# Inverse roots of two norms: from small products and a chain on VectorE to a sum by ones and ScalarE's reciprocal root

## The chip, the cores and the metric

The kernel runs on one core of a Trainium2 chip. The metric is the device time of one launch in microseconds (us), as the median of several runs. The profile is one more execution, recorded by the hardware profiler; its time stands beside the others below.

A core has a matrix engine (TensorE, PE in the profile, with its weight loads as PEld), an elementwise engine (VectorE, DVE), a function engine (ScalarE, ACT), GpSimd (POOL) and SyncE (SP), whose queue issues most of the DMAs here. TensorE writes into PSUM, eight banks of 128 partitions by 512 float32 columns. Each engine works through a queue of its own in order, and waits on semaphores where it needs another's result.

## The reference, cut to what matters

A decoder layer over 2048 tokens of width 1024: a norm, a mixing part (a gated recurrence in four heads beside sliding-window attention), an output projection, a second norm, a gated feed-forward part of width 2816 with a short convolution, and a final norm.

```python
def rmsnorm(x, w, eps=EPS):
    xf = x.astype(jnp.float32)
    inv = lax.rsqrt(jnp.mean(xf * xf, axis=-1, keepdims=True) + eps)
    return (xf * inv * w.astype(jnp.float32)).astype(x.dtype)
...
        h = h + mix @ w_out[l]
        v = rmsnorm(h, norm_ffn_w[l])
        gate = causal_depthwise_conv(v @ w_gate[l], conv_w[l], conv_b[l])
        h = h + (jax.nn.silu(gate) * (v @ w_up[l])) @ w_down[l]
    return rmsnorm(h, final_norm_w)
```

The inverse root "inv" is one number for each token. It is computed for x, for h (after the mixing part) and for the result (the final norm).

## The kernel before, in words

**Layout.** Activations are kept transposed: features on the 128 partitions, tokens along the columns. A token's inverse root therefore multiplies a whole column, and has to stand on all 128 partitions.

**Order of the work.** The tokens are done in two halves of 1024 (hf 0 and 1). Each half runs the mixing part, then `out_proj` (products "pop"), `gate_up` (11 pairs of feature tiles, a gate pair and an up pair each) and `down`. Large products are made in float32r, each factor split into a high and a low part, with three products in place of one; the splits are a cast on ScalarE and a subtraction on VectorE (L721 and L722, or L195 and L196). The feed-forward products use a seven-product scheme for 2x2 blocks: `pair_unit` makes the products A11, A12, S2, S1, S3, S4 and A22 and gathers them in the banks X, Z and Y. X and Y take up further products on top of what they hold, so each is first copied away by ScalarE ("s", "u", L903). Usually the order is A11 into X, A12 into Z, S2 on top of X. The very first gate pair of a half, which follows on `out_proj`, has the order A11, A12, S1, S2, S4, S3, A22, and a new X for A22.

**The planner.** The program is written as tiles and operations, and a planner orders the instructions in each engine's queue by readiness and the order in the program, and hands out the buffers. What stands later in the code may run earlier. A name such as "mm" is a ring of buffers: PSUM has four banks "mm", two "hg" and two "at". The ring "ut" has seven buffers of 128x512 float32 in SBUF.

**Sums of squares.** `Stats` gathers the squares of a stage's tiles in an accumulator `acc`, one partial sum per partition and token. `inverse` (L258 on) makes inverse roots from it: for each 128 tokens a product with the 128x128 block of `acc` as weights and one column of ones as the moving operand sums over the partitions; the sums land with tokens on partitions, in a few columns of a bank "hg" (tile pst, L271). On these, 128x8 or 128x4 elements, `rsqrt` (L164 on) runs eleven small VectorE operations: a scaled copy, a first guess from the bits, three Newton steps of three operations. Then one VectorE operation (L279) writes a diagonal matrix per 128 tokens into `acc`. `spread` (L281 on) multiplies 512 columns of these diagonals by a 128x128 matrix of ones (tile pinv, L289, banks "hg" and "at" in turn) which puts each inverse root on all partitions, and ScalarE copies it to `acc` (L292).

**Where they are used.** `load` and `head` make them for x (tile invb). `gate_up` makes those of h: `inverse` at the product S4 of the first gate pair, `spread` at A22, and the pending multiplications of the gate by invb (L962, `flush`) behind that. `down` makes those of the final norm, in two parts of 512 tokens: "o2" for the upper and "o" for the lower ones (tile sums in the first half). In the first half o2's `inverse` stands at the second piece of the last product P4 and its `spread` two pieces later, with `finish`, which multiplies eight tiles (L1201) and writes them out; o's `inverse` stands in the unit "kv" that already belongs to the second half, and its `spread` and `finish` in the next unit. In the second half the loop ends before these points, and the tail computes o2 and o (in two parts of 256) in its own way.

Of the kernel before, what the change touches and what calls it, by code (L numbers as in the profile page):

```python
# [8 lines left out]
F32 = mybir.dt.float32  # L9
# [3 lines left out]
AF = mybir.ActivationFunctionType  # L13
ALU = mybir.AluOpType
# [3 lines left out]
P = 128  # L18
D = 1024
# [11 lines left out]
EPS = 1e-6  # L31
# [9 lines left out]
UT = 7  # L41
# [12 lines left out]
def hymba_layer(ctx: ExitStack, tc: tile.TileContext, a: dict, out: bass.AP):  # L54
    nc = tc.nc
# [17 lines left out]
    def ps(kind, name):  # L73
        return spaces[kind].tile([P, 512], F32, tag=kind, name=name)

    aux = ("hg", "at")
# [7 lines left out]
    ones = cp.tile([P, P], F32, name="ones")  # L84
    nc.vector.memset(ones, 1.0)
    warm, eps = [t[:, i:i + 1] for t in [cp.tile([P, 2], F32, name="warm")] for i in range(2)]
# [148 lines left out]
    class Stats:  # L235
# [26 lines left out]
        def inverse(self, keep, last=None):  # L262

            n = self.acc.shape[-1]
            nt = n // P
            st = ps("hg", "pst")

            for src in (self.acc, last):
                if src is not None:
                    for c in range(nt):  # L270
                        marks["pst"] = nc.tensor.matmul(st[:, c:c + 1], src[:, c * P:(c + 1) * P], ones[:, 0:1],  # L271
                                                        start=src is self.acc and (c == 0 or last is None),
                                                        stop=last is None or src is last,
                                                        skip_group_check=last is not None)
            if last is not None:
                without_use(ps("at", "idle"), TAIL_WARM, marks["pst"])
            rs = self.rs = rsqrt(st[:, 0:nt], nt, 1.0 / D, keep, last is not None)
            dg = self.acc
            return nc.vector.tensor_tensor(dg.rearrange("p (c t) -> p c t", t=P),  # L279
                                    ident.unsqueeze(1).to_broadcast([P, nt, P]),  # L280
                                    rs.unsqueeze(2).to_broadcast([P, nt, P]), op=ALU.mult)  # L281

        def spread(self, bank=None):

# [113 lines left out]
    def first_unit(X, i, then={}, kind="mm"):  # L398
        return unit(a["w_att"][ATT_J + i], X, "kv", kind=kind, then=then)
# [544 lines left out]
    def gate_up(hf, ops, hs, nxt, last, p):  # L944

        acts = {op: [dp.tile([P, n, 512], F32, name=f"act{hf}{op}{i}") for i, n in enumerate(PIECES)] for op in OPS}
        lo, hi = slice(0, 512), slice(512, HALF)
        invb = hs.acc
        srcs = [w[2 * pr:2 * pr + 2] for pr in range(FT // 2) for w in (a["w_gate"], a["w_up"])]
        for pr in range(FT // 2):  # L950
            f0 = 2 * pr
            W, nxt = nxt, None

            ga = [p.tile([P, HALF + 64], F32, tag="ga", name="ga", bufs=2)[:, 0:2 + HALF] for _ in range(2)]

            def gate(i, j, x, y):
                dst = ga[i][:, 2 + j * 512:2 + (j + 1) * 512]
                iv = invb[:, j * 512:(j + 1) * 512]
                if y is not None:
                    nc.vector.tensor_tensor(dst, x, y, op=ALU.add)  # L960
                    x = dst
                later.append(lambda: nc.vector.tensor_tensor(dst, x, iv, op=ALU.mult))  # L962
                if pr:
                    flush()

            def flush():
                while later:
                    later.pop(0)()

            later = []  # L970
            then = {"S4": lambda: hs.inverse("h"), "A22": lambda: (hs.spread(), flush())} if pr == 0 else {}
            if pr == 0:
                def behind_first(copied):
                    nonlocal nxt
                    with behind(*last(copied)):
                        nxt = prep_pair(srcs[1][0], srcs[1][1])

                pair_unit(W, ops, p, gate, then, behind_first)
            else:
                nxt = prep_pair(srcs[2 * pr + 1][0], srcs[2 * pr + 1][1])  # L980
                pair_unit(W, ops, p, gate, then)
            flush()
            ys = []
            for i in range(2):
                ft, g = f0 + i, ga[i]
                nc.scalar.copy(g[:, 0:2], halo[:, ft])
                nc.scalar.copy(halo[:, ft], g[:, HALF:HALF + 2])
                y = slot("y")
                nc.scalar.activation(y, g[:, 2:2 + HALF], AF.Identity, scale=C.cw[:, ft, 2:3], bias=C.cw[:, ft, 3:4])  # L989
                for w in (1, 0):  # L990
                    nc.vector.scalar_tensor_tensor(y, g[:, w:w + HALF], C.cw[:, ft, w:w + 1], y,  # L991
                                                   op0=ALU.mult, op1=ALU.add)
                nc.scalar.activation(y, y, AF.Silu)
                nc.vector.tensor_tensor(y, y, invb, op=ALU.mult)
                ys.append(y)

            def up(i, j, x, y):
                dst = ys[i][:, j * 512:(j + 1) * 512]
                if y is not None:
                    nc.vector.tensor_tensor(y, x, y, op=ALU.add)  # L1000
                    x = y
                nc.vector.tensor_tensor(dst, x, dst, op=ALU.mult)

            W = nxt
            if pr + 1 < FT // 2:
                nxt = prep_pair(srcs[2 * pr + 2][0], srcs[2 * pr + 2][1])
            pair_unit(W, ops, p, up)

            y1, y2 = ys
            dst = {op: acts[op][pr // 2][:, pr % 2] for op in OPS}  # L1010
            tt = slot("T13")
            nc.sync.dma_start(dst["B11"], y1[:, lo])
            nc.sync.dma_start(dst["B21"], y2[:, lo])
            nc.sync.dma_start(dst["B22"], y2[:, hi])
            nc.vector.tensor_tensor(tt[:, lo], y1[:, hi], y1[:, lo], op=ALU.subtract)
            nc.sync.dma_start(dst["T1"], tt[:, lo])
            nc.vector.tensor_tensor(tt[:, hi], y2[:, hi], y1[:, hi], op=ALU.subtract)
            nc.sync.dma_start(dst["T3"], tt[:, hi])
            nc.vector.tensor_tensor(y1[:, lo], tt[:, hi], y1[:, lo], op=ALU.add)
            nc.sync.dma_start(dst["T2"], y1[:, lo])  # L1020
            nc.vector.tensor_tensor(y2[:, lo], y2[:, lo], y1[:, lo], op=ALU.subtract)
            nc.sync.dma_start(dst["T4"], y2[:, lo])
        return acts

    def down(hf, kept, acts, p):
# [4 lines left out]
        lo, hi = slice(0, 512), slice(512, HALF)  # L1030
        final = hf + 1 == NH
        NP = len(PIECES)
        todo = [(name, w, t, j) for name, w, t in PRODUCTS for j in range(NP)]
        S = {}

# [44 lines left out]
        hh = []  # L1080
# [32 lines left out]
        X, xs, acc = [], None, None  # L1113
        end = len(todo) - NP
        for k, (name, _, _, j) in enumerate(todo):
            if k + 2 < len(todo):
                ready[k + 2] = prep_piece(k + 2)
            if j == 0:
# [4 lines left out]
                else:  # L1123
                    o = by if name == "P3" else bx
                if name == "P3":
                    acc = inv_tile() if final else wp.tile([P, HALF], F32, tag="raw", name="sums", bufs=RAW)
                    s1, s2 = [Stats(acc[:, bs], lambda: p.tile([P, 512], F32, tag="ut", name="fsq", bufs=UT))
                              for bs in (lo, hi)]
# [3 lines left out]
            if not final and k >= end - 3:  # L1132
                xs = next(loading, xs)
            if final and k == end:
                break
            if k == end + 1:
                s2.inverse("o2")
            elif k == end + 3:
                s2.spread()
                finish(hf, hh, s2, hi, [nc.sync])  # L1140
            for d in range(4):
                product(k, o[d], d)
            if j + 1 < NP:
                continue
# [18 lines left out]
        if final:  # L1163
# [4 lines left out]
            for i, (st, bs) in enumerate(steps):  # L1168
                for d in range(4):
                    for k in range(end, len(todo)):  # L1170
                        product(k, bx[d][:, bs], d, bs)
                    t = hh[d + 4][:, bs]
# [17 lines left out]
            steps[1][0].inverse("o", last)  # L1190
            finish(hf, hh, steps[1][0], steps[1][1], [nc.scalar, nc.sync], steps[1][0].spread(1))
            return None
        kv = [first_unit(X, 0, {3: lambda: s1.inverse("o"), 7: lambda: xs.inverse("x")}, "aux")]
        kv.append(first_unit(X, 1, {2: lambda: (s1.spread(), finish(hf, hh, s1, lo, [nc.sync])), 4: xs.spread}))
        f0 = unit(a["w_f"][0], X, "f")
        return X, kv, xs.acc, xs.rs, f0

    def finish(hf, hh, st, bs, queues, inv=None):
        for d in range(KT):
            t = hh[d][:, bs]  # L1200
            nc.vector.tensor_tensor(t, t, st.acc if inv is None else inv, op=ALU.mult)  # L1201
            queues[d % len(queues)].dma_start(out[d, :, hf * HALF + bs.start:hf * HALF + bs.stop], t)

    X = []
    *nxt, summed = X, *head(X)
    for hf in range(NH):
        X, kv, invb, rs, f0 = nxt
        with ExitStack() as st:
            p = pool(f"mix{hf}", stack=st, reuse_waits="tile")
# [25 lines left out]
        with ExitStack() as st:  # L1235
            p = pool(f"ffn{hf}", stack=st, reuse_waits="tile")
            kept, ops, hs, first, last = out_proj(hf, M, p)
# [63 lines left out]
```

## Time and profile before

| | |
|---|---|
| runs | 2151.5, 2153.11, 2151.62 us; median 2151.62 |
| the profiled execution | 2152.56 us, span 2150.8 us |
| granted clock of TensorE | 0.999 |
| instructions | 28224 |
| matrix products on pst (L271), records | 100: 80 from invb, 16 from sums, 4 from fsq |
| matrix products on pinv (L289), records | 26: 22 from invb, 4 from sums |
| spread's copy on ScalarE (L292) | 11 of 128x512 |
| table loads of ScalarE | 33 of 1283 ns |

The span runs from the first to the last instruction. A row of a timeline has the start in us, the length in us, the engine, the line of the code, the operation, output and inputs, shapes and a count; what stands in brackets is the idle time before it and what ended it. Products overlap, so the length of one (0.39 us for 128x512) is more than the distance to the next. A float32 product (one that isn't float32r) leaves two records. In a table of stretches the columns are the stretch, its length, the busy time and the number of instructions of PE, PEld, DVE, ACT and POOL, the granted clock, the share of the DMA engines and GB/s. In a table of groups stand the busy time, the mean length of one in ns, and the idle time before them with what ended it.

### The profile page before, as it was taken

How to read it: one execution, taken by the hardware profiler on the slowest of the kernel's cores; microseconds unless marked ns; L12 is line 12 of the kernel's file. 1: busy time of each engine (PE TensorE's matmuls, PEld its weight loads, DVE VectorE, ACT ScalarE, POOL GpSimd, SP SyncE). 2: the span in 40 equal slices, each digit the busy share in tenths (PEclk: the TensorE clock that was granted, in tenths of full speed). 3: DMA queues.
4: the chain of work that ended last, by engine and by line, in shares of the span. 5: the costliest groups of instructions: out<-in, count | busy, mean ns of one | idle time of the engine just before them, and what ended most of it. 6: DMA issues, size and time to landing. Idle time of an engine off the chain costs nothing.

```text
span 2150.8 us, 28224 instructions
## 1 busy us (share of the span) xinstructions
PE 2136.1 (99%) x10752; PEld 1786.6 (83%) x10752; DVE 1662.3 (77%) x2450; ACT 1091.3 (51%) x1858; POOL 6.0 (0%) x28
## 2 busy tenths in 40 slices
PE   9999999999999999999999999999999999999998
PEld 7888888888888888888888888888888888888888
DVE  6557888798887878785864688878978788887766
ACT  6456566564444445335734576646544444443353
POOL 1000000000000000000000000000000000000000
PEclk9999999999999999999999999999999999999999
DMA  4111112513232235964631111215223323269643
GB/s 158 49 40 40 42 37 69 164 48 132 86 126 93 97 114 171 380 222 157 214 129 41 46 42 40 64 38 174 84 93 101 110 91 122 92 205 398 224 137 133
DMA packets 94383, 258.04 MB, mean 120 GB/s; under 512 B 11416, under 2 KB 17576, under 8 KB 94248
## 3 DMA queue, kind: packets, MB, share of 16 engines
q1 hardware_dynamic: 88992, 251.30, 34.5%
q10 hardware_dynamic: 5256, 4.94, 0.8%
q8 instruction: 84, 1.38, 0.3%
q14 instruction: 51, 0.42, 0.1%
HBM read 195.10 MB, written 57.15 MB: 117 GB/s over the span
## 4 chain that ended last, share of the span: by engine, by line
PE 79%; ACT 2%; DVE 2%; issue 1%; DMA 0%; ACTq 0%; DVEq 0%
PE X L896 7%; PE X L898 7%; PE X L897 7%; PE pop L217 6%; PE pdx L1109 4%; PE pdx L1107 4%; PE Y L898 4%; PE Y L897 4%; PE Y L896 4%; PE pdx L1108 4%; PE pdy L1109 3%; PE pdy L1108 3%; PE pdy L1107 3%; PE f L217 2%; PE hq L217 2%; PE q L217 2%
## 5 line engine op out<-in xcount | busy, mean ns | idle before, releaser
L721 ACT CAST whi<-raw 128x1024 fp32r<-128x1024 f32 x88 | 92.6, 1053 | 110.3 <-PE X L897 67.6
L897 PE MATMUL X<-T,whi 128*128 128x512 f32 x352 | 137.0, 389 | 0.0
L896 PE MATMUL X<-T,whi 128*128 128x512 f32 x352 | 137.0, 389 | 0.0
L898 PE MATMUL X<-T,wlo 128*128 128x512 f32 x352 | 136.9, 389 | 0.0
L991 DVE SCALAR_TENSOR_TENSOR y<-ga,cw,y 128x1024 f32<-128x1024 f32 x88 | 112.3, 1277 | 26.0 <-ACT y L989 25.9
L903 ACT COPY u<-X 128x512 f32<-128x512 f32 x88 | 51.4, 584 | 133.0 <-PE X L898 132.6
L722 DVE TENSOR_TENSOR wlo<-raw,whi 128x1024 fp32r<-128x1024 f32 x88 | 107.0, 1215 | 0.0
L195 ACT CAST whi<-raw 128x1024 fp32r<-128x1024 f32 x57 | 59.7, 1051 | 87.1 <-PE hq L217 37.1
L196 DVE TENSOR_TENSOR wlo<-raw,whi 128x1024 fp32r<-128x1024 f32 x57 | 69.4, 1217 | 43.3 <-ACT whi L195 42.8
L722 DVE TENSOR_TENSOR xld<-raw,xhd 128x1024 fp32r<-128x1024 f32 x72 | 80.5, 1129 | 19.8 <-ACT xhd L721 19.4
L721 ACT CAST xhd<-raw 128x1024 fp32r<-128x1024 f32 x72 | 69.6, 977 | 43.5 <-DMA raw<-act0T 13.9
L217 PE MATMUL pop<-XL,whi 128*128 128x512 f32 x256 | 88.6, 392 | 0.0
L217 PE MATMUL pop<-XH,wlo 128*128 128x512 f32 x256 | 87.7, 391 | 0.0
L217 PE MATMUL pop<-XH,whi 128*128 128x512 f32 x256 | 86.4, 393 | 0.0
L897 PEld LDWEIGHTS X<-T,whi 128*128 128x128 f32 x352 | 66.1, 188 | 13.7
L898 PEld LDWEIGHTS X<-T,wlo 128*128 128x128 f32 x352 | 66.1, 188 | 13.7
L896 PEld LDWEIGHTS X<-T,whi 128*128 128x128 f32 x352 | 66.0, 188 | 13.7
L1107 PE MATMUL pdx<-xhd,hid 128*128 128x512 f32 x192 | 74.5, 392 | 1.6 <-ACT hid L721 1.0
L619 DVE TENSOR_TENSOR QK<-QK,f 128x1024 f32<-128x1024 f32 x56 | 68.5, 1224 | 8.1 <-ACT G L605 7.7
L1108 PE MATMUL pdx<-xld,hid 128*128 128x512 f32 x192 | 74.7, 389 | 0.0
L1109 PE MATMUL pdx<-xhd,lod 128*128 128x512 f32 x192 | 73.8, 389 | 0.0
L896 PE MATMUL X<-T,Sh 128*128 128x512 f32 x176 | 68.7, 391 | 1.5 <-ACT s L903 1.5
(385 smaller groups left out, 6413.1 us busy)
## 6 DMA issues: line engine op xcount, KB each, us to landing
wr<-in_w_down SPq DMA_DIRECT2D x90, 512.0 KB, 5.4
raw<-in_w_gate SPq DMA_DIRECT2D x44, 512.0 KB, 3.7
raw<-in_w_up SPq DMA_DIRECT2D x44, 512.0 KB, 3.6
raw<-act0T SPq DMA_DIRECT2D x20, 512.0 KB, 8.2
raw<-act1T SPq DMA_DIRECT2D x20, 512.0 KB, 8.3
act0B<-y SPq DMA_DIRECT2D x33, 256.0 KB, 3.2
act1B<-y SPq DMA_DIRECT2D x33, 256.0 KB, 2.3
raw<-in_w_out SPq DMA_DIRECT2D x16, 512.0 KB, 5.1
```

The source lines that it names most:

```text
L196: nc.vector.tensor_tensor(lo, raw, hi.bitcast(F32), op=ALU.subtract)
L217: marks["unit"] = nc.tensor.matmul(o[b], w, x[:, bs], start=f, stop=l)
L619: done = nc.vector.tensor_tensor(own, own, Fv.rearrange("p b w -> p w b").unsqueeze(3).to_broadcast([P, 2, nb, m]), op=ALU.mult)
L721: return (nc.scalar.copy(h, src), (eng or nc.vector).tensor_tensor(l, src, h.bitcast(F32), op=ALU.subtract))
L722: (eng or nc.vector).tensor_tensor(l, src, h.bitcast(F32), op=ALU.subtract))
L896: nc.tensor.matmul(o, wh[:, ws], xh, start=i == 0 and not more, stop=False, skip_group_check=more)
L897: nc.tensor.matmul(o, wh[:, ws], xl, start=False, stop=False, skip_group_check=more)
L898: r = nc.tensor.matmul(o, wl[:, ws], xh, start=False, stop=i == 3, skip_group_check=more)
L991: nc.vector.scalar_tensor_tensor(y, g[:, w:w + HALF], C.cw[:, ft, w:w + 1], y, op0=ALU.mult, op1=ALU.add)
L1107: nc.tensor.matmul(o, wh[:, i, c], ah[:, i, cols], start=f, stop=False, skip_group_check=more)
L1108: nc.tensor.matmul(o, wh[:, i, c], al[:, i, cols], start=False, stop=False, skip_group_check=more)
L1109: nc.tensor.matmul(o, wl[:, i, c], ah[:, i, cols], start=False, stop=l, skip_group_check=more)
```

## The change

A new function `everywhere` of `Stats` takes the place of `inverse` and `spread` at h (both halves) and at o2 and o (first half). For each 512 columns it multiplies `acc` itself by the 128x128 ones, in float32, so that the sum over the partitions stands on all partitions at once. ScalarE makes a reciprocal root of it with scale and eps; VectorE scales the sums, and one Newton step follows: a square on ScalarE and two VectorE operations, the last of which writes the inverse root into `acc`. The two work tiles come from the ring "ut". The banks are "mm" for h, and "hg" for o2 and o.

```diff
+        def everywhere(self, part, kinds):
+
+            n = self.acc.shape[-1]
+            for b in range(n // 512):
+                a = self.acc[:, b * 512:(b + 1) * 512]
+                s = ps(kinds[b % 2], "psum")
+                nc.tensor.matmul(s, ones, a, start=True, stop=True)
+                y, t = part("y"), part("t")
+                nc.scalar.activation(y, s, AF.Abs_reciprocal_sqrt, scale=1.0 / D, bias=eps)
+                nc.vector.tensor_scalar(a, s, -0.5 / D, -0.5 * EPS, op0=ALU.mult, op1=ALU.add)
+                nc.scalar.activation(t, y, AF.Square)
+                nc.vector.tensor_tensor(t, t, a, op=ALU.mult)
+                nc.vector.scalar_tensor_tensor(a, t, 1.5, y, op0=ALU.add, op1=ALU.mult)
...
+        def ring(name):
+            return p.tile([P, 512], F32, tag="ut", name=name, bufs=UT)
...
-            then = {"S4": lambda: hs.inverse("h"), "A22": lambda: (hs.spread(), flush())} if pr == 0 else {}
+            then = {"S4": lambda: hs.everywhere(ring, ("mm", "mm")), "A22": flush} if pr == 0 else {}
...
             if k == end + 1:
-                s2.inverse("o2")
+                s2.everywhere(ring, aux)
             elif k == end + 3:
-                s2.spread()
                 finish(hf, hh, s2, hi, [nc.sync])
...
-        kv = [first_unit(X, 0, {3: lambda: s1.inverse("o"), 7: lambda: xs.inverse("x")}, "aux")]
-        kv.append(first_unit(X, 1, {2: lambda: (s1.spread(), finish(hf, hh, s1, lo, [nc.sync])), 4: xs.spread}))
+        kv = [first_unit(X, 0, {3: lambda: s1.everywhere(ring, aux), 7: lambda: xs.inverse("x")}, "aux")]
+        kv.append(first_unit(X, 1, {2: lambda: (finish(hf, hh, s1, lo, [nc.sync])), 4: xs.spread}))
```

The inverse roots of x, and the second half's final norm, keep `inverse` and `spread`.

More of the change, by code (lines that the diff above doesn't have):

```diff
@@ L1032, in down, with ring @@
         NP = len(PIECES)
+        def ring(name):
+            return p.tile([P, 512], F32, tag="ut", name=name, bufs=UT)
         todo = [(name, w, t, j) for name, w, t in PRODUCTS for j in range(NP)]
```

## The prediction

> **What bounds the kernel now.** I read the busy times of the page first, then the table of stretches, then the waits of TensorE, then its timeline around each place that the change touches.
>
> ```profile
> PE 2136.1 (99%) x10752; PEld 1786.6 (83%) x10752; DVE 1662.3 (77%) x2450; ACT 1091.3 (51%) x1858; POOL 6.0 (0%) x28
> 440.00:480.00 40.00, 39.27 (x177) 31.74 (x176) 35.33 (x56) 21.94 (x35) 0.00 (x0) 1.00 0.13 40
> 875.00:1040.00 165.00, 165.00 (x729) 136.64 (x728) 112.30 (x117) 74.86 (x85) 0.00 (x0) 1.00 0.68 247
> 1040.00:1112.00 72.00, 72.00 (x329) 58.65 (x328) 60.59 (x103) 40.36 (x52) 0.00 (x0) 1.00 0.54 180
> PE X L896 <- ACT s L903: 1.5, 2, 0.7
> ```
>
> TensorE is busy in all of 875 to 1040: 729 products in 165 us, one every 226 ns. Between 440 and 480 it loses 0.73 us, and the row of waits names the reason: twice in the run the up-product on bank X waits 0.7 us for ScalarE's copy "s". Whatever leaves TensorE's queue in such a stretch should come off the span. VectorE is the engine to watch: 35.33 of 40 us in the first place of the change, 60.59 of 72 in the other.
>
> **What is removed from TensorE.** Four inversions change: h in each half, o2 and o in the first. Those of x and of the second half's final norm stay. For each changed one the products on pst go (eight for h, four for o2 or o; each stands as two records), and the products on pinv stay as products of the same shape, 128x512 float32 by ones, only now on the raw sums. In the chain of waits the pieces are:
>
> ```profile
> 447.67 1.68 PE pst L271 x16
> 463.71 1.72 PE pinv L289 x4
> 1046.09 0.79 PE pst L271 x8
> 1083.05 0.79 PE pst L271 x8
> 1513.11 1.68 PE pst L271 x16
> ```
>
> All four pst pieces lie on the chain that ends last. By these rows 1.68 + 0.79 + 0.79 + 1.68 = 4.94 us go; the 1.72 us of pinv per h (0.43 a record) remains. The timeline says a little more, because the first product after pst is slow too:
>
> ```profile
> 447.28 0.39 PE L897 MATMUL Y<-B,S 128*128 128x512 f32 x1
> 447.51 1.84 PE L271 MATMUL pst<-ones,invb 128*128 128x1 f32 x16
> 449.21 0.49 PE L898 MATMUL Y<-B,S 128*128 128x512 f32 x1
> 449.53 0.40 PE L896 MATMUL Y<-B,S 128*128 128x512 f32 x1
> 1045.70 0.39 PE L1109 MATMUL pdx<-xh2d,lod 128*128 128x512 f32 x1
> 1046.73 0.49 PE L1107 MATMUL pdx<-xh2d,hid 128*128 128x512 f32 x1
> 1047.06 0.40 PE L1108 MATMUL pdx<-xl2d,hid 128*128 128x512 f32 x1
> ```
>
> From the start at 447.28 to that at 449.53 are 2.25 us, where two products at 0.226 would take 0.45: pst costs 1.80. At 1045.70 to 1047.06 it is 1.36 less 0.45, so 0.91. Twice each: 5.42 us. The direct term lies between 4.94 and 5.42.
>
> **The stall behind h.** The up-pair normally runs A11 into X, A12 into Z, then S2 on top of X, so that Z covers the copy of X. In the pair behind h the order is another:
>
> ```profile
> 459.55 0.39 PE L898 MATMUL X<-B,wlo 128*128 128x512 f32 x1
> 460.67 0.50 PE L896 MATMUL X<-T,Sh 128*128 128x512 f32 x1 [0.73 <-ACT s L903]
> 461.00 0.40 PE L897 MATMUL X<-T,Sh 128*128 128x512 f32 x1
> 463.55 1.88 PE L289 MATMUL pinv<-invb,ones 128*128 128x512 f32 x4
> 464.86 0.80 PE L896 MATMUL Z<-B,whi 128*128 128x512 f32 x1
> ...
> 460.03 0.58 ACT L903 COPY s<-X 128x512 f32<-128x512 f32 x1 [1.43 <-PE X L898]
> ...
> 461.24 1.23 DVE L279 TENSOR_TENSOR invb<-ident,y 128x1024 f32<-128x1024 f32 x1
> ```
>
> S2 comes straight after A11, and Z directly after pinv. In the code spread takes its banks from "hg" and "at", and Z is the next tile from "at": I read it so that Z's bank is handed out only after pinv's, and pinv needs VectorE's multiply, which ends at 462.5. The changed h takes both banks from "mm" and takes them 16 us earlier, at the place of pst, where the sums are done. Nothing then holds Z back, and its 2.7 us (twelve products at 0.226) lie over the copy of 0.58. What goes is 461.00 - 459.55 - 0.45 = 1.00 us by starts, 0.73 by the wait alone; twice, so 1.46 to 2.00. Below: nothing, if the order stays. I take it as gone.
>
> "mm" has four banks: X of A11, the two sums, and X of A22 fill them, and the fifth request, X of the up-pair at 457, takes the first X, which ScalarE's "u" copy of 454.59 frees in the trace of before. The sums' banks are asked for again only in the next pair, about 20 us on. I cost the bank change at nothing.
>
> **What is added on VectorE and ScalarE.** For each 512 columns VectorE gets three operations over 128x512, ScalarE a reciprocal root from PSUM and a square, and it loses the copy of pinv. The reciprocal root is in no row; its neighbours are these:
>
> ```profile
> L716 ACT ACTIVATE v<-pvv,y 128x512 f32<-128x512 f32 x16 | 11.0, 688 | 34.8 <-PE pvv L715 34.8
> L248 ACT ACTIVATE sq<-h 128x512 f32<-128x512 f32 x28 | 16.3, 622 | 0.7 <-DVE h L786 0.7
> L993 ACT ACT_TABLE_LOAD x2 | 2.6, 1283 | 0.0
> L786 DVE TENSOR_TENSOR h<-h,pop 128x512 f32<-128x512 f32 x32 | 20.4, 680 | 7.5 <-DMA h<-in_xT 6.2 <-PE pop L217 1.3
> 454.59 0.59 ACT L903 COPY u<-X 128x512 f32<-128x512 f32 x1 [4.99 <-PE X L898]
> ```
>
> For h, ScalarE's new work is a table load of 1.28 us at most (nothing, if the function shares a set with its neighbours), two roots at about 0.69 and two squares at 0.62: 3.9 us. It has a hole of 4.99 us just there, before 454.59, after the sums can be ready (447.5 + 1.72 = 449.2). The hole hides it; without it the copies "u" and "s" would be up to 3.9 us late.
>
> VectorE gets six operations at 0.68 (0.60 from start to start, 3.6 to 4.1 us) and loses eleven small ones and the 1024-wide multiply:
>
> ```profile
> 450.32 0.15 DVE L169 TENSOR_SCALAR ms<-pst 128x8 f32<-128x8 f32 x1
> 456.50 1.22 DVE L722 TENSOR_TENSOR Sl<-S,Sh 128x1024 fp32r<-128x1024 f32 x1
> 461.04 0.17 DVE L181 SCALAR_TENSOR_TENSOR y<-t,y 128x8 f32<-128x8 f32 x1
> 465.22 2.50 DVE L962 TENSOR_TENSOR ga<-ga,invb 128x512 f32<-128x512 f32 x4 [2.75 <-ACT invb L292]
> ```
>
> The small ones run from 450.32 to 461.2, squeezed between large ones, and the inverse is everywhere only at 465.22, with VectorE idle 2.75 us before it. The new chain is shorter: sums at 449.2, root and square by about 453, the last two VectorE operations by 456 to 458. So the gate multiplies move some 8 us ahead, and VectorE's hole at 462.5 fills. Net it works about 1 us more per h. What could be late is the split Sl: done at 457.7, and its first product is the third of S2, two after 460.67 at 461.2; with Z ahead, pst and the stall gone it starts at 461.2 + 2.7 - 1.8 - 1.0 = 461.1, so 3.4 us of room against at most 4.1 added ahead of it, less five small ones (0.1 each between large ones), and only if all six go ahead of Sl. I take nothing for it, and keep it for the slower rival.
>
> **o2 and o, at the end of the first half.** Per call three VectorE operations (2.0 us) for eleven small ones and a multiply of 0.68, and on ScalarE 1.3 us for one copy, with one table load for both calls. TensorE reads pieces split two ahead, so some us of delay are covered. The step that moves is the finish of o2: eight multiplies with their eight output DMAs on SP's queue.
>
> ```profile
> 1066.65 1.23 DVE L196 TENSOR_TENSOR wlo<-raw,whi 128x1024 fp32r<-128x1024 f32 x1 [0.26 <-ACT whi L195]
> 1070.53 0.68 DVE L1093 TENSOR_TENSOR h<-h,pdx 128x512 f32<-128x512 f32 x1
> 1071.36 0.39 PE L217 MATMUL kv<-XH,whi 128*128 128x512 f32 x1
> ...
> 1078.70 4.90 DVE L1201 TENSOR_TENSOR h<-h,sums 128x512 f32<-128x512 f32 x8 [0.76 <-ACT sums L292]
> ...
> 441.00:455.00 14.00, 14.00 (x71) 11.86 (x70) 13.50 (x23) 6.79 (x14) 0.00 (x0) 1.00 0.14 38
> 1057.00:1071.00 14.00, 14.00 (x64) 11.59 (x63) 12.66 (x19) 8.71 (x9) 0.00 (x0) 1.00 0.51 178
> ```
>
> They start at 1078.70 before the change and could start near 1057, where VectorE was busy 12.66 of the 14 us to 1071. Behind them stands wlo for kv, done at 1067.9 and needed with kv's fifth product, 1071.36 + 4 x 0.226 = 1072.3. Room: 4.4 us, against 4.9 us moved less the small operations that go. I take nothing, and keep this as a rival. The output DMAs move with them; the weight loads behind them on SP's queue (f, q) feed products some 20 us later.
>
> **Sum.** Direct 4.94 to 5.42, stall 1.46 to 2.00: 6.4 to 7.4, middle 6.9. The profiled execution took 2152.56 us for a span of 2150.8, so it would come to 2145.7; it lies 0.94 above the median of the runs, 2151.62, and from that 6.9 gives **2144.7**. The likeliest case by itself: 2143.8 to 2146.2, with half a microsecond for a changed order at other places; the second half's stretches are bound by TensorE too, so a saving in the first half passes through.
>
> One rule speaks against it. The Trainium skill, page "Perfetto Trace Analysis", section "Identifying the Most-Contended Engine", says that busy time of matmuls is no good measure of headroom and that the busy share of weight loads is to be used with the flop rate. By weight loads alone TensorE is at 83%, has slack, and the sum would be near nothing. The trace disagrees in this kernel: in 875 to 1040 the loads take 136.64 of 165 us, yet a product starts every 226 ns without a wait.
>
> **Rivals.**
>
> 1. The stall stays (Z or X still out of order). Then only pst goes: 4.94 to 5.42, 2146.2 to 2146.7. Against it: Z follows pinv at once. Chance 0.14.
>
> 2. A wait that replaces the removed one: o2's finish pushes wlo for kv behind the four adds that begin at 1070.53 and what follows them. The loss is 1 to 4.9 us (the length of the moved block), so 2145.7 to 2149.6, mostly over 2147.3. For it: the room is 4.4 against up to 4.9. Against: the multiplies may wait as they do now. Chance 0.16.
>
> 3. TensorE isn't the limit there, by weight loads or because a VectorE chain elsewhere ends at the same time as before: 2150 to 2152. VectorE at 35.33 of 40 speaks for it, TensorE at 72.00 of 72 against. Chance 0.10.
>
> 4. Slower. In h, VectorE's queue stands at its multiply by the square, which waits for ScalarE's load, roots and square, with Sl and the other splits queued behind. Of Sl's room of 3.4 us the added work takes up to 3.6 if all six operations go ahead of it (4.1 less five small ones at 0.1), so nothing is left, and each us of waiting then stops TensorE, once per half. To turn 6.9 us of gain into a loss of 4.3 it must stop for 5.6 per half: a wait of 5.6 us is the point from which it decides. At 6.5 us the time is 2151.62 - 6.9 + 2 x 6.5 = 2157.7. ScalarE's work in front is 3.9 us in a hole of 4.99, which speaks against it; VectorE busy in 13.50 of the 14 us from 441 to 455 speaks for it. Chance 0.10.
>
> **How the numbers follow.** Forecast 0.50, rivals 0.14, 0.16, 0.10, 0.10. I count as faster what is under 2147.3 (0.2% is 4.3 us, about what a measurement of this kernel can tell from no change). The forecast and rival 1 lie there, and a quarter of rival 2: 0.50 + 0.14 + 0.04 = 0.68. Within 0.2%: 0.12 of rival 2 and rival 3: 0.22. Slower: 0.10. The range takes in the forecast and rivals 1 and 2, 0.80 together: 2142.6 (the full 7.4, and 1.6 more, as far as the three runs before lie apart, 2151.5 to 2153.11) to 2149.8.
>
> **What would show it.** In the profile after: no pst on invb at h, nor on sums in the first half; four records of 0.43 on the new sums near 447; Z between the two X products and the wait of X on "s" gone; ScalarE's table loads up by three or fewer in the whole run; the gate multiplies before 460. Wrong would be a wait of TensorE for wlo or Sl near 460 or 1072, or VectorE idle behind the new square. The forecast fails if TensorE's busy time falls by 5 us and its idle time grows by as much.

## The result, and the profile after

The changed kernel takes 2161.07 us (median of 6 runs, 2160.38 to 2163.1) against 2151.8 (6 runs, 2151.5 to 2153.11): a ratio of 1.0042 [1.003, 1.0053]. It is slower by 9.3 us, where 6.9 less was predicted. The profiled execution took 2163.1 us, with a span of 2161.4 and a granted clock of 0.999, as before.

The page and its table of stretches come first. Of before, only the row from 480 to 840 was not shown yet:

```profile
480.00:840.00 360.00, 360.00 (x1590) 298.08 (x1590) 298.87 (x383) 156.28 (x227) 0.00 (x0) 1.00 0.33 108
```

And these are the rows of after:

```profile
PE 2147.0 (99%) x10704; PEld 1781.7 (82%) x10704; DVE 1664.7 (77%) x2420; ACT 1097.6 (51%) x1867; POOL 6.0 (0%) x28
...
440.00:480.00 40.00, 40.00 (x172) 31.95 (x171) 36.68 (x51) 26.06 (x40) 0.00 (x0) 1.00 0.13 40
480.00:840.00 360.00, 360.00 (x1568) 293.90 (x1567) 297.15 (x380) 154.76 (x224) 0.00 (x0) 1.00 0.33 107
875.00:1040.00 165.00, 165.00 (x722) 135.32 (x721) 111.43 (x117) 71.87 (x82) 0.00 (x0) 1.00 0.67 244
1040.00:1112.00 72.00, 71.47 (x316) 57.89 (x315) 58.17 (x80) 39.76 (x48) 0.00 (x0) 1.00 0.60 198
```

TensorE has 48 records fewer and is busy 10.9 us longer (2147.0 against 2136.1). It isn't waiting: span less busy time is 14.4 us, and was 14.7. The stretch from 480 to 840 lies in gate pairs and up pairs that the change doesn't touch. TensorE is busy in all of it both times, at a clock of 1.00, yet 1568 products fit where 1590 did. That is 229.6 ns from start to start in place of 226.4. **Products that the change leaves alone cost more**, those in 875 to 1040 too (722 for 729).

The timeline of after shows where it sets in, at the first gate pair of the first half:

```profile
435.95 0.39 PE L217 MATMUL pop<-XH,whi 128*128 128x512 f32 x1
436.18 0.39 PE L217 MATMUL pop<-XL,whi 128*128 128x512 f32 x1
436.41 0.39 PE L217 MATMUL pop<-XH,wlo 128*128 128x512 f32 x1
436.63 0.40 PE L910 MATMUL X<-B,whi 128*128 128x512 f32 x1
436.87 0.39 PE L911 MATMUL X<-B,whi 128*128 128x512 f32 x1
437.09 0.40 PE L912 MATMUL X<-B,wlo 128*128 128x512 f32 x1
437.33 0.39 PE L910 MATMUL X<-B,whi 128*128 128x512 f32 x1
437.56 0.40 PE L911 MATMUL X<-B,whi 128*128 128x512 f32 x1
437.80 0.39 PE L912 MATMUL X<-B,wlo 128*128 128x512 f32 x1
```

The same products before:

```profile
436.17 0.39 PE L896 MATMUL X<-B,whi 128*128 128x512 f32 x1
...
437.30 0.39 PE L898 MATMUL X<-B,wlo 128*128 128x512 f32 x1
```

From the first product on B to the sixth are 1.17 us after and 1.13 before, that is 234 and 226 ns each. The products on pop ahead of them keep their pitch. At 436.63 none of the new instructions has run yet; the first product on the new sums comes at 448.41. So neither their work nor a wait of theirs can be the reason, only something that the change does to the whole program.

One such thing stands in the code: the results of the old inverse roots were kept under names of their own (eight columns for "h", four for "o"), and these two names are no longer allocated. Each had two buffers of 32 bytes in the pool "small", so 128 bytes go, and **every tile allocated behind that pool lies 128 bytes lower** on each partition. The first tile of the feed-forward pool starts at byte 140992, before at 141120. The pools ahead of it (x, weights, h) stay where they were. In the first gate pair the moving operand B moves, the weights whi and wlo don't.

To see what goes with the pitch I matched the trace's products one by one with the program's, in order (10704 records after, 10752 before), took the addresses of each one's moving operand and weights, and grouped the distances from start to start of neighbouring float32r products over 512 columns by these addresses modulo 256 (distances of 215 to 250 ns, so that waits stay out):

```
kernel   moving  weights  next weights   count   mean ns
before     64      64         64          8029    227.0
after      64      64         64          5753    227.6
after     192      64         64          1744    232.6
after      64     192        192           396    232.8
after     192     192        192           108    228.2
```

Where the moving operand and the weights lie alike, the pitch is about that of before; where they are 128 apart, it is 232.6 to 232.8. The excess over 227.0 in these rows is 5753 x 0.6 + 1744 x 5.6 + 396 x 5.8 + 108 x 1.2 ns = 15.6 us. In these groups a product's own weights and those of the next one lie alike, so they can't say which of the two counts; small groups, of 23 to 48 pairs, in which only one of the two is apart from the moving operand, lie at 231.8 to 234.2 ns as well. The cost was found in the trace and has to be tested: the addresses can be moved alone.

### The profile page after: what moved, and what is told of

The parts are those of the page before. It is cut to its first block, busy times and chain, and to the rows that moved or that the text cites. A ratio compares the mean times of both kernels' runs of the same rounds, so it can differ in the third digit from the quotient of the medians.

```text
span 2161.4 us, 28119 instructions
## 1 busy us (share of the span) xinstructions
PE 2147.0 (99%) x10704; PEld 1781.7 (82%) x10704; DVE 1664.7 (77%) x2420; ACT 1097.6 (51%) x1867; POOL 6.0 (0%) x28
## 4 chain that ended last, share of the span: by engine, by line
PE 78%; ACT 2%; DVE 2%; DMA 1%; issue 1%; ACTq 0%; DVEq 0%
PE X L911 7%; PE X L910 7%; PE X L912 7%; PE pop L217 6%; PE Y L911 4%; PE Y L910 4%; PE Y L912 4%; PE pdx L1128 3%; PE pdx L1130 3%; PE pdx L1129 3%; PE pdy L1128 3%; PE pdy L1129 3%; PE pdy L1130 3%; PE f L217 2%; PE hq L217 2%; PE q L217 2%
## 5 line engine op out<-in xcount | busy, mean ns | idle before, releaser
L911 PEld LDWEIGHTS X<-T,whi 128*128 128x128 f32 x352 | 66.1, 188 | 14.4
L911 PE MATMUL Z<-B,whi 128*128 128x512 f32 x176 | 69.5, 395 | 0.0
```

The costliest lines, as they stand in the source:

```text
L911: nc.tensor.matmul(o, wh[:, ws], xl, start=False, stop=False, skip_group_check=more)
```

## The experiments

Two theories stood against each other: **addresses** (the change saves what was predicted, and 128 bytes cost more than that) and **operations** (the change's own instructions disturb TensorE).

### 1. Put the tiles back, and move them without the change

e1 is the changed kernel with 128 bytes given back behind the pool "small". e2 is the kernel before with the same line, so that its tiles move by 128 bytes upward. In e3 the line stands ahead of all pools, so that all tiles move alike; e4 is e2 with 256 bytes.

```diff
-    sp = pool("small", bufs=2)
+    sp = pool("small", bufs=2); pool("pad").tile([P, 32], F32, name="pad")
```

> The changed kernel with 128 bytes per partition left empty behind the pool of small tiles. The change took two tags out of that pool, so all later tiles (those of the mixing and feed-forward stages) lie 128 bytes lower; this puts them back where they lay before, in the same order of instructions. Theory (address): products whose moving operand and weights lie 128 apart modulo 256 take 232.6 ns from start to start against 227.0, 2323 of them after the change against 70 before; 2253 x 5.6 ns = 12.6 us go, and up to 16 us if the smaller rise of the others (227.0 to 227.6) goes too: 2144.8 to 2148.5 us. Rival (work): the new operations of ScalarE and VectorE, or new waits, cost the time: stays at 2161.

> The kernel before, with 128 bytes left empty at the same place: no other change. Address theory: 2324 products become slow by 5.6 ns, 2151.8 + 12.6 to 16 = 2164 to 2168 us. Rival (work): no change, 2151.8.

> The kernel before, with 128 bytes left empty ahead of all tiles, so that every tile moves by 128 bytes and the distances between them stay. If the distance between the two operands of a product decides: no change, 2151.8 us within 1.5. If the place itself decides (64 or 192 modulo 256): most of the 8200 float32r products become slow, 8200 x 5.6 ns = 46 us, some 2198 us.

> The kernel before, with 256 bytes left empty behind the pool of small tiles. If the distance counts modulo 256: no change, 2151.8 us within 1.5. If any move of the later tiles costs, or the distance counts modulo 512 or more: slower, by up to the 12 to 16 us of the 128 bytes.

Measured, with 2152.03 for the kernel before on that chip: e1 2145.84, ratio 0.9972 [0.9962, 0.9983]; e2 2167.67, 1.0075 [1.0061, 1.0089]; e3 2151.82, 0.9999 [0.999, 1.0008]; e4 2151.93, 1.0 [0.9991, 1.0009].

The page's busy row and the table of stretches of e1, then the stretch of e2:

```profile
PE 2130.1 (99%) x10704; PEld 1780.9 (83%) x10704; DVE 1665.3 (78%) x2420; ACT 1099.6 (51%) x1867; POOL 6.4 (0%) x28
...
480.00:840.00 360.00, 360.00 (x1590) 298.20 (x1589) 298.99 (x383) 156.47 (x227) 0.00 (x0) 1.00 0.33 110
```

```profile
480.00:840.00 360.00, 360.00 (x1567) 293.93 (x1567) 295.92 (x379) 154.82 (x224) 0.00 (x0) 1.00 0.32 106
```

With the same instructions as after, in the same order, e1 has 1590 products in this stretch again, and TensorE is busy 16.9 us less than after. With the same instructions as before, in the same order, e2 has the 1567 of after. Between after and e1 lie 15.2 us (2161.07 - 2145.84), between e2 and before 15.6. e3 says that no single place is slow: with operands and weights at 192 modulo 256, 8029 pairs have 227.0 ns. e4 says that the pad as such and a distance of 256 cost nothing. Addresses it is; operations would have left e1 slow and e2 as before.

### 2. How the cost goes with the distance

e8 and e9 are e2 with 64 and 32 bytes (`[P, 16]`, `[P, 8]`). e10 puts the 128 bytes behind the pool x, so that all tiles behind it move, the weights among them. The tiles in x, which are moving operands (XH, XL, xhd and others), stay, and so do the constants ahead of them.

```diff
-    xp = pool("x")
+    xp = pool("x"); pool("pad").tile([P, 32], F32, name="pad")
```

> The kernel before with 64 bytes left empty behind the small tiles: 2165 products have their operands 64 (or 192) apart modulo 256. If any distance other than 0 modulo 256 costs the same 5.6 ns and its tail: 2165 to 2168 us, as with 128. If only 128 is bad: 2152. If the cost grows with the distance: between.

> The kernel before with 32 bytes left empty behind the small tiles: 2143 products have their operands 32 (or 224) apart modulo 256. If any distance but 0 costs about 5 to 6 ns, as 64 and 128 did: 2164 to 2168 us. If a distance under 64 stays within one unit of the memory: 2152.

> The kernel before with 128 bytes left empty between the tiles of x and the weights, so that all tiles but those of x move. Distance theory: 6435 of the 8300 wide float32r products, those with a moving operand among the tiles of x, become slow by 5.6 ns: 2152 + 36, near 2188 us, also in the mixing stage. Rival (the place of the feed-forward tiles alone decides): as e2, 2168.

Measured: e8 2165.4, ratio 1.0062 [1.0049, 1.0076]; e9 2170.59, 1.0087 [1.0073, 1.01]; e10 2186.02, 1.016 [1.0146, 1.0174]. In e10 the mixing part slows down too; a stretch of its second half in the table of before, and then in that of e10:

```profile
1200.00:1360.00 160.00, 160.00 (x1012) 136.79 (x1011) 126.46 (x232) 100.29 (x237) 0.00 (x0) 1.00 0.14 40
```

```profile
1200.00:1360.00 160.00, 160.00 (x976) 136.17 (x975) 119.84 (x225) 96.25 (x223) 0.00 (x0) 1.00 0.14 42
```

The same matching gives for the pairs that are apart:

```
kernel  moving  weights  count  mean ns      alike: count  mean ns
e8       128      64      1740    230.4             5748    228.1
e8        64     128       396    233.5               92    227.0
e9        96      64      1740    233.5             5748    227.9
e9        64      96       396    233.1               92    227.7
e10       64     192      5853    232.5             1876    227.9
e10      192      64       362    232.4
```

Every tried distance that is no multiple of 256 costs, 32 bytes no less than 128 (18.4 us in e9, over its forecast, against 15.6 in e2), and the cost grows with the number of products that are apart, though not in proportion: some 2100 in e2, e8 and e9 for 13 to 18 us, 6200 in e10 for 34. By the excess over 227.0 in these rows e10 should lose 5853 x 5.5 + 362 x 5.4 + 1876 x 0.9 ns = 35.8 us; it lost 33.9.

### 3. The parts of the change, with the tiles in place

e5 makes the change at h alone, e6 at o2 and o alone; each drops one of the two names, so 64 bytes are put back. e7 is e1 with the two sums of h in the banks "hg" and "at", which pinv had before, in place of "mm".

```diff
-                s2.everywhere(ring, aux)
+                s2.inverse("o2")
...
+                s2.spread()
...
-        kv = [first_unit(X, 0, {3: lambda: s1.everywhere(ring, aux), 7: lambda: xs.inverse("x")}, "aux")]
-        kv.append(first_unit(X, 1, {2: lambda: (finish(hf, hh, s1, lo, [nc.sync])), 4: xs.spread}))
+        kv = [first_unit(X, 0, {3: lambda: s1.inverse("o"), 7: lambda: xs.inverse("x")}, "aux")]
+        kv.append(first_unit(X, 1, {2: lambda: (s1.spread(), finish(hf, hh, s1, lo, [nc.sync])), 4: xs.spread}))
```

> The change at h alone (both halves); o2 and o as before; the later tiles held at their old place (64 bytes empty). Theory of the prediction's sum: eight products on pst go twice (3.4 to 3.6 us) and the stall on the copy s goes twice (1.5 to 2.0): 2152.0 - 4.9 to 5.6, 2146.4 to 2147.1 us. Rival: the stall isn't what h gives, and only 3.4 to 3.6 go: 2148.5.

```diff
-            then = {"S4": lambda: hs.everywhere(ring, ("mm", "mm")), "A22": flush} if pr == 0 else {}
+            then = {"S4": lambda: hs.inverse("h"), "A22": lambda: (hs.spread(), flush())} if pr == 0 else {}
```

> The change at o2 and o alone; h as before; the later tiles at their old place. Sum of the prediction: 1.6 to 1.8 us go, 2150.2 to 2150.4. With the wait of kv for wlo that the padded changed kernel shows (0.7 us): 2150.9 to 2151.1. If the moved finish costs more: no change or slower, 2152 or above.

```diff
-            then = {"S4": lambda: hs.everywhere(ring, ("mm", "mm")), "A22": flush} if pr == 0 else {}
+            then = {"S4": lambda: hs.everywhere(ring, aux), "A22": flush} if pr == 0 else {}
```

> The changed kernel with the padding of 128 bytes, but h takes its two banks from hg and at instead of mm. If Z was late before because pinv itself came late: Z keeps its place, 2145.8 us as with mm. If taking a bank of Z's ring at all holds Z back: the stall returns twice, 2147.3 to 2147.8 us.

Measured, against 2151.98 for before: e5 2146.97, ratio 0.9975 [0.9965, 0.9984], so -5.0 us (3.4 to 7.5); e6 2151.35, 1.0001 [0.9992, 1.001]; e7 2147.06, 0.9976 [0.9966, 0.9987], which can't be told from e1, nor by the time alone from the rival's 2147.3 to 2147.8. e5's interval reaches its rival's 3.4 to 3.6 us too. So the lists of waits have to decide on the stall. The waits of TensorE in e6, where h is as before:

```profile
PE X L910 <- ACT s L917: 1.5, 2, 0.7
...
PE kv L217 <- DVE wlo L196: 0.5, 1, 0.5
```

The stall of X on "s" is there with h's old code and in no list of waits with the new, in e5 and e7 neither. So sharing the ring "at" isn't enough to hold Z back: with "hg" and "at" again, but early, the stall stays away. What is left is that pinv came late. Whether Z then stood behind it because of the bank or only because of the order of the queue isn't shown: no run puts a late pinv into other banks.

### 4. More of the same, and the finish of o2 behind

e11 carries the change to o2 of the second half too, 320 bytes put back. e12 is e11 with the first half's finish of o2 moved into the unit "kv".

```diff
-                        s2.inverse("o2")
+                        s2.everywhere(ring, aux)
...
-                        s2.spread()
```

> The changed kernel with the later tiles at their old place (320 bytes empty), and o2 of the second half made by everywhere as well: four products on pst less (0.9 us), one table load of ScalarE more in a stretch where TensorE works. Theory: 2145.8 - 0.9 = 2144.9. Rival: the chain behind the last product, and not TensorE, sets the end there: 2145.8.

```diff
-            elif k == end + 3:
-                finish(hf, hh, s2, hi, [nc.sync])
...
-        kv = [first_unit(X, 0, {3: lambda: s1.everywhere(ring, aux), 7: lambda: xs.inverse("x")}, "aux")]
+        kv = [first_unit(X, 0, {0: lambda: finish(hf, hh, s2, hi, [nc.sync]), 3: lambda: s1.everywhere(ring, aux), 7: lambda: xs.inverse("x")}, "aux")]
```

> As e11, and in the first half the finish of o2 stands behind the split of kv's weights instead of two pieces earlier. Theory: the wait of kv for wlo (0.7 us in e1) goes, 2144.2. Rival: the finish only pushes other splits, and nothing changes against e11: 2144.9.

Measured, against 2152.17 for before: e11 2147.43, ratio 0.9979 [0.997, 0.9988]; e12 2146.72, 0.9976 [0.9966, 0.9985]. Neither gains on e1, and both lie above either of their forecasts. In the waits of e11 the removed products come back as a wait in the tail:

```profile
PE pst L271 <- ACT fsq L257: 2.1, 1, 2.1
```

The same row of e1:

```profile
PE pst L271 <- ACT fsq L257: 0.6, 1, 0.6
```

These are the last sums of the tail, which wait for ScalarE's squares. TensorE's timeline and the stretch of its end, for e1 and then for e11:

```profile
2133.58 0.50 PE L271 MATMUL pst<-ones,invb 128*128 128x1 f32 x4
2134.71 0.61 PE L271 MATMUL pst<-ones,fsq 128*128 128x1 f32 x4 [0.62 <-ACT fsq L257]
2135.18 1.81 PE L99 MATMUL idle<-ones 128*128 128x128 f32 x14
...
2135.00:2140.00 5.00, 2.68 (x19) 2.09 (x19) 3.39 (x13) 0.46 (x2) 0.00 (x0) 1.00 0.31 104
```

```profile
2132.68 0.50 PE L271 MATMUL pst<-ones,invb 128*128 128x1 f32 x4
2135.26 0.60 PE L271 MATMUL pst<-ones,fsq 128*128 128x1 f32 x4 [2.08 <-ACT fsq L257]
2135.73 2.94 PE L99 MATMUL idle<-ones 128*128 128x128 f32 x14
...
2135.00:2140.00 5.00, 4.26 (x20) 3.54 (x20) 1.67 (x8) 0.98 (x3) 0.00 (x0) 0.66 0.30 104
```

TensorE comes to these sums 0.9 us sooner, and the squares are ready 0.55 us later, so it waits 1.5 us longer. Behind the longer wait the granted clock is 0.66 in place of 1.00, and the products without use that follow (idle, L99) take 2.94 us in place of 1.81. That is how e11, with fewer products, ends after e1 in these traces.

In e12 kv's wait for wlo is 0.5, against 0.3 in e11 and 0.7 in e1. It doesn't test its theory: `finish` stands behind the split in the code, but the planner still put its eight multiplies ahead of wlo in VectorE's queue.

```profile
1061.46 4.90 DVE L1218 TENSOR_TENSOR h<-h,sums 128x512 f32<-128x512 f32 x8
...
1068.61 1.21 DVE L196 TENSOR_TENSOR wlo<-raw,whi 128x1024 fp32r<-128x1024 f32 x1
```

Of the kernels run, **e1 has the lowest median**, 6.2 us under before and 15.2 under the change as made; e5, e7, e11 and e12 lie within the interval of its gain.

## Why the prediction was wrong, by its own steps

**The step that failed** is the sum itself: it takes the time before, subtracts what goes, and so lets all remaining products keep their 226 ns from start to start. That the removed tiles hold 128 bytes, and that all later tiles move with them, has no term in it. By the runs this term is +15.2 us (after against e1), more than twice the rest. The range reached to 2149.8 and left it out.

**The mechanism of the saving was right at h, and isn't shown at o2 and o.** With the tiles in place the change gives -6.2 us (e1), with an interval of 3.7 to 8.2, against 6.4 to 7.4 predicted. Point by point:

- *pst and the stall at h*: 2 x 1.80 and 1.46 to 2.00 were predicted, 5.1 to 5.6 together; e5 gave 5.0. Of after, the chain of waits holds the new sums (L289 of that kernel) with no pst beside them:

```profile
448.41 1.72 PE psum L289 x4
...
1519.05 1.72 PE psum L289 x4
```

- *The order behind h*: the timeline of after shows Z between A11 and S2, as foretold:

```profile
460.73 0.40 PE L912 MATMUL X<-B,wlo 128*128 128x512 f32 x1
460.96 0.39 PE L912 MATMUL Z<-B,wlo 128*128 128x512 f32 x1
...
463.76 0.39 PE L910 MATMUL X<-T,Sh 128*128 128x512 f32 x1
...
464.23 0.39 PE L912 MATMUL X<-T,Sl 128*128 128x512 f32 x1
...
461.16 0.59 ACT L917 COPY s<-X 128x512 f32<-128x512 f32 x1 [0.71 <-PE X L912]
```

  The 3.03 us from 460.73 to 463.76 lie over the copy "s". My reading of the cause (Z's bank handed out after pinv's) stays open: e7 takes the old banks early and has no stall either, so the new banks weren't needed.

- *o2 and o*: 0.91 twice, 1.8 us, were predicted. e6 shows 0.6 between the medians, and its interval, up to 1.7 us faster and 2.2 slower, tells it neither from that nor from nothing. Part of it goes the way of rival 2. The timelines of VectorE and TensorE after:

```profile
1070.98 4.90 DVE L1221 TENSOR_TENSOR h<-h,sums 128x512 f32<-128x512 f32 x8
...
1078.12 1.22 DVE L196 TENSOR_TENSOR wlo<-raw,whi 128x1024 fp32r<-128x1024 f32 x1
...
1077.80 0.62 PE L217 MATMUL kv<-XH,whi 128*128 128x512 f32 x2
...
1079.40 0.73 PE L217 MATMUL kv<-XH,wlo 128*128 128x512 f32 x2 [0.53 <-DVE wlo L196]
```

  The eight multiplies do stand ahead of wlo now, and kv waits for it. Measured from kv's first product, wlo ends 5.0 us later than before (1.54 us after that product in place of 3.48 ahead of it). The room of 4.4 us covers most of this, so the wait is 0.5 us and not the 1 to 4.9 of that rival, which ran up to the length of the whole block. The room itself was misread by a little: before, the third product of kv needed wlo, not the fifth.

```profile
1071.81 0.39 PE L217 MATMUL kv<-XH,wlo 128*128 128x512 f32 x1
```

  That leaves 3.9 us before; after, kv's two banks take turns, and it is the fifth.

- *VectorE and ScalarE at h*: cover was predicted to suffice, and did. The group of the new table loads, then the timelines of ScalarE and VectorE, after:

```profile
L291 ACT ACT_TABLE_LOAD x3 | 3.8, 1283 | 0.7 <-PE psum L289 0.7
...
449.35 1.28 ACT L291 ACT_TABLE_LOAD   x1 [0.69 <-PE psum L289]
450.64 0.69 ACT L291 ACTIVATE y<-psum,warm 128x512 f32<-128x512 f32 x1
...
451.36 0.69 DVE L292 TENSOR_SCALAR invb<-psum 128x512 f32<-128x512 f32 x1 [0.49 <-ACT y L291]
...
460.31 1.21 DVE L736 TENSOR_TENSOR Sl<-S,Sh 128x1024 fp32r<-128x1024 f32 x1
461.45 0.68 DVE L295 SCALAR_TENSOR_TENSOR invb<-t,y 128x512 f32<-128x512 f32 x1
462.05 1.22 DVE L736 TENSOR_TENSOR wlo<-raw,whi 128x1024 fp32r<-128x1024 f32 x1
463.19 1.28 DVE L980 TENSOR_TENSOR ga<-ga,invb 128x512 f32<-128x512 f32 x2
```

  The root takes 0.69 us, the value taken, with a table load at three places (o needs none behind that of o2). Sl ends at 461.52, and its first product, in the rows of TensorE above, starts at 464.23. The end of the chain was placed wrong: its last VectorE operation, foretold by 456 to 458, ends at 462.13, because VectorE's queue puts S, raw and Sl between the Newton steps. So the gate multiplies, foretold 8 us ahead and before 460, start at 463.19, 2 us ahead of 465.22. TensorE's list of waits shows none for them.

**The rivals.** Rival 4 had the sign, slower, by a mechanism that didn't happen: TensorE never waits for Sl, and VectorE waits 0.49 us there. Rival 1 (stall stays) is out, rival 3 (TensorE isn't the limit) too. The Trainium skill's rule behind rival 3, page "Perfetto Trace Analysis", section "Identifying the Most-Contended Engine", says to judge TensorE's headroom by the flop rate and the busy share of weight loads. That share is 83% in before and in e1, and yet e1 is faster by about what left TensorE's queue. In the tail of the second half something like rival 3 holds: e11 takes more off TensorE and gains nothing.

What I had written as the sign of failure, busy time down by 5 and idle time up by as much, did not come either. Busy time itself went up, in a stretch where nothing had been changed: that is the sign to look for.

## What to carry to other kernels

An edit that adds or drops even a small tile moves every tile allocated behind it; before a change is judged by its time, compare the addresses of moving operands and weights, or hold them in place with a pad. Where a profile slows down in a stretch that the edit doesn't touch, count the products per stretch at full clock before looking for a wait. A TensorE-bound kernel in float32r is worth laying out so that moving operands and weights start at the same offset modulo 256.

## What the runs showed of the hardware

Float32r products over 128x512 whose moving operand and weights start at the same byte modulo 256 on a partition follow each other at 227 to 228 ns; at distances of 32, 64 and 128 the means of the large groups are 230.4 to 233.5 ns. The place itself doesn't matter (e3), nor a distance of 256 (e4). The Trainium skill, page "SBUF — State Buffer", section "A bandwidth-pool intuition that's wrong (but worth ruling out)", gives TensorE a second, independent read port for its weights. By that the two would not disturb each other; these runs differ with it by some 5.6 ns a product at 128 bytes, and the measurement decides. What in the memory makes the difference isn't shown, nor why products that lie alike take 0.6 to 1.1 ns more in a program in which others are apart. No distance of a few bytes and no other type was tried.
